# RMSNorm and SiLU on 64 tiles: float32 tiles on one SyncE queue, Square and Silu on ScalarE, rstd by a power on GpSimd

**Chip, cores, metric.** One core of one Trainium2 chip. The metric is the device time of one execution in microseconds; a kernel's figure is the median of its runs. Engines are named as the profile names them: ACT is ScalarE, DVE is VectorE, POOL is GpSimd, SP is SyncE.

## The reference

```python
# x: (8, 1024, 2048) float32, gamma: (2048,) float32, eps = 1e-5
rms = np.sqrt(np.mean(x ** 2, axis=-1, keepdims=True) + eps)
out = gamma * x / rms
return (out * (1 / (1 + np.exp(-out)))).astype(np.float32)
```

Both kernels cut the 8192 rows into 64 tiles of 128 rows (one per partition) by 2048, 1 MiB each in HBM.

## The kernel before

POOL issues every DMA, and the DMA casts between float32 in HBM and bf16 in SBUF (the page counts 512 KB for a load and 1024 KB for a store; HBM reads 68.16 MB and writes 67.11). DVE multiplies by gamma and sums squares, ACT takes the root, DVE the reciprocal, ACT the Silu. (In the cuts of code here `...` and left-out lines, such as the allocation of small tiles, stand in full in the kernel.)

```python
    pool = ctx.enter_context(tc.tile_pool(name="pool", bufs=8))
    ...
    for i in range(ntiles):
        xt = pool.tile([P, d], bf16)
        nc.gpsimd.dma_start(out=xt[:ts], in_=x2[s:e])          # casts
        xg = pool.tile([P, d], bf16)
        nc.vector.tensor_mul(out=xg[:ts], in0=xt[:ts], in1=g[:ts])
        nc.vector.tensor_tensor_reduce(...)                     # ss = sum of squares
        nc.scalar.activation(out=rms[:ts], in_=ss[:ts], func=Sqrt, ...)
        nc.vector.reciprocal(out=rstd[:ts], in_=rms[:ts])
        ot = pool.tile([P, d], bf16)
        nc.scalar.activation(out=ot[:ts], in_=xg[:ts], func=Silu, scale=rstd[:ts])
        nc.gpsimd.dma_start(out=o2[s:e], in_=ot[:ts])          # casts back
```

## Time and profile before

| | kernel before |
|---|---|
| time, median | 339.02 us (337.41 to 339.48, 4 runs) |
| span of the profile | 336.1 us |

The lines of the profile, and how I read them, are in the prediction. In short, the DMA bounds this kernel: the packets of its one queue fill 104% of sixteen engines' span, and no compute engine passes 66%.

### The profile page before, as it was taken

The page shows a single profiled execution, that of the slowest core. Times are in us where ns is not written, and L with a number is a line of the kernel's source. Part 1 is how long each engine was busy: PE and PEld are TensorE (multiplying, and loading weights), DVE is VectorE, ACT ScalarE, POOL GpSimd, SP SyncE. Part 2 cuts the span into 40 slices and gives each one's busy share as a digit, 9 for nine tenths or more (in the row PEclk, how much of TensorE's full clock was granted, in tenths as well). Part 3 has the DMA queues.
Part 4 walks back from the last instruction along what each step waited for, and adds up shares of the span by engine and source line. Part 5 has one row for each costly group of instructions (what it writes and reads, how often), then busy time and mean ns, then how long its engine had stood idle before and what let it go on. Part 6 is the DMA issues. An engine that isn't in the chain of part 4 may idle for free.

```text
span 336.1 us, 838 instructions
## 1 busy us (share of the span) xinstructions
DVE 221.2 (66%) x257; ACT 219.1 (65%) x188; POOL 69.0 (21%) x133
## 2 busy tenths in 40 slices
DVE  0999990407999914099999030899991308999900
ACT  1486977522869795238697761386978613869792
POOL 6012111050111110501111105011111050111110
DMA  7999999899999998999999989999999799999997
GB/s 140 212 214 254 335 398 363 332 312 208 214 288 327 402 365 321 324 214 214 291 316 414 366 325 310 214 212 319 307 424 367 286 297 214 213 311 309 420 429 273
DMA packets 18582, 101.24 MB, mean 301 GB/s; under 512 B 2064, under 2 KB 2064, under 8 KB 10384
## 3 DMA queue, kind: packets, MB, share of 16 engines
q0 software_dynamic: 18576, 101.20, 104.1%
q14 instruction: 6, 0.05, 0.0%
HBM read 68.16 MB, written 67.11 MB: 402 GB/s over the span
## 4 chain that ended last, share of the span: by engine, by line
issue 72%; POOL 14%; DMA 11%; POOLq 1%; PEldq 0%
DMA xt<-in_x_dram 11%; POOL out_dram L65 10%; POOL xt L42 4%; POOLq L65 0%; POOL g L34 0%; POOLq L96 0%; POOLq L42 0%; PEldq L96 0%
## 5 line engine op out<-in xcount | busy, mean ns | idle before, releaser
L48 DVE CUSTOM_DVE_ANT_0 xt<-xt 128x2048 bf16<-128x2048 bf16 x64 | 144.8, 2280 | 0.3
L45 DVE TENSOR_TENSOR xg<-xt,g 128x2048 bf16<-128x2048 bf16 x64 | 76.6, 1217 | 95.7 <-DMA xt<-in_x_dram 95.7
L62 ACT ACTIVATE ot<-xg,rstd 128x2048 bf16<-128x2048 bf16 x64 | 124.4, 1993 | 5.8 <-DVE rstd L59 5.5
L55 ACT ACTIVATE rms<-ss,eps_t 128x1 f32<-128x1 f32 x64 | 17.8, 292 | 101.8 <-DVE ss L48 63.7
L65 POOL DMA_DIRECT2D out_dram<-ot x64 | 34.2, 534 | 221.4 <-ACT ot L62 221.4
L42 POOL DMA_DIRECT2D xt<-in_x_dram x64 | 34.1, 554 | 38.8 <-DVE ss L48 22.8
L55 ACT ACT_TABLE_LOAD x30 | 38.5, 1283 | 2.1 <-DVE ss L48 1.0
L62 ACT ACT_TABLE_LOAD x30 | 38.5, 1283 | 0.5
L59 DVE RECIPROCAL rstd<-rms 128x1 f32<-128x1 f32 x64 | 8.6, 153 | 8.4 <-ACT rms L55 8.4
L48 DVE DVE_READ_ACCUMULATOR2_ANT ss<- 128x1 f32 x64 | 5.2, 81 | 0.0
L34 POOL DMA_DIRECT2D g<-in_gamma_dram x1 | 0.7, 667 | 0.8 <-PEq L96 0.8
L36 DVE MEMSET eps_t<- 128x1 f32 x1 | 0.1, 59 | 0.8 <-PEq L82 0.8
L82 POOL MEMSET const-float32-0.0<- 128x1 f32 x1 | 0.1, 99 | 0.2 <-issue 0.2
L82 POOL MEMSET const-bfloat16-1.0<- 128x1 bf16 x1 | 0.1, 102 | 0.0
L82 POOL MEMSET const-float32-1.0<- 128x1 f32 x1 | 0.1, 99 | 0.0
L82 POOL MEMSET const-uint8-127<- 128x1 uint8 x1 | 0.1, 99 | 0.0
## 6 DMA issues: line engine op xcount, KB each, us to landing
out_dram<-ot POOLq DMA_DIRECT2D x64, 1024.0 KB, 11.5
xt<-in_x_dram POOLq DMA_DIRECT2D x64, 512.0 KB, 15.5
g<-in_gamma_dram POOLq DMA_DIRECT2D x1, 512.0 KB, 4.7
```

The costliest lines, as they stand in the source:

```text
L34: nc.gpsimd.dma_start(out=g, in_=gbc)
L36: nc.vector.memset(eps_t, float(eps))
L42: nc.gpsimd.dma_start(out=xt[:ts], in_=x2[s:e])
L45: nc.vector.tensor_mul(out=xg[:ts], in0=xt[:ts], in1=g[:ts])
L48: nc.vector.tensor_tensor_reduce(out=xt[:ts], in0=xt[:ts], in1=xt[:ts], scale=1.0, scalar=0.0, op0=mybir.AluOpType.mult, op1=mybir.AluOpTy ...
L55: nc.scalar.activation(out=rms[:ts], in_=ss[:ts], func=mybir.ActivationFunctionType.Sqrt, scale=1.0 / d, bias=eps_t[:ts])
L59: nc.vector.reciprocal(out=rstd[:ts], in_=rms[:ts])
L62: nc.scalar.activation(out=ot[:ts], in_=xg[:ts], func=mybir.ActivationFunctionType.Silu, scale=rstd[:ts])
L65: nc.gpsimd.dma_start(out=o2[s:e], in_=ot[:ts])
L82: nc = _bacc.Bacc("TRN2", target_bir_lowering=False, num_devices=1)
```

## The change

The intent: keep the DMA engines full from end to end. Tiles stay float32, no DMA casts, and SyncE issues them all; 23 buffers are worked on in place; 16 loads run ahead; Square with a running sum replaces DVE's sum; the root becomes a power of -0.5 on POOL, so ACT loads no Sqrt table between two Silus (the kernel before has 60 table loads of 1.283 us, the changed one two). The text keeps Square two tiles ahead of Silu.

```diff
-        nc.gpsimd.dma_start(out=xt[:ts], in_=x2[s:e])
...
+    BUFS, LEAD = 23, 16
+    def load(i):
+        xt = pool.tile([P, d], f32, name="xt")
+        nc.sync.dma_start(out=xt, in_=x2[i * P:(i + 1) * P])
+        xts[i] = xt
...
+    nc.gpsimd.partition_broadcast(g, grow)        # gamma: one row, then all partitions
...
+    def stats(i):
+        nc.scalar.activation(out=sq, in_=xts[i], func=ACT.Square, accum_out=ss)
+        nc.gpsimd.tensor_scalar(out=var, in0=ss, scalar1=1.0 / d, scalar2=float(eps),
+                                op0=ALU.mult, op1=ALU.add)
+        nc.gpsimd.tensor_tensor(out=rstd, in0=var, in1=half, op=ALU.pow)
+    def scale(i):
+        nc.vector.scalar_tensor_tensor(out=xts[i], in0=xts[i], scalar=rstds.pop(i), in1=g,
+                                       op0=ALU.mult, op1=ALU.mult)
+    def finish(i):
+        nc.scalar.activation(out=xt, in_=xt, func=ACT.Silu)
+        nc.sync.dma_start(out=o2[i * P:(i + 1) * P], in_=xt)
+        if i + LEAD < ntiles:
+            load(i + LEAD)
+    for i in range(ntiles + 2):
+        if i < ntiles:
+            stats(i)
+        if 0 <= i - 1 < ntiles:
+            scale(i - 1)
+        if i >= 2:
+            finish(i - 2)
```

More of the change, by code (lines that the diff above doesn't have):

```diff
@@ L7 @@
 from concourse._compat import with_exitstack
+ACT = mybir.ActivationFunctionType
+ALU = mybir.AluOpType
 @with_exitstack
@@ L25 @@
     n, d = x2.shape
-    ntiles = (n + P - 1) // P
+    ntiles = n // P
+    BUFS, LEAD = 23, 16
     singles = ctx.enter_context(tc.tile_pool(name="singles", bufs=1))
-    pool = ctx.enter_context(tc.tile_pool(name="pool", bufs=8))
+    pool = ctx.enter_context(tc.tile_pool(name="pool", bufs=BUFS))
     small = ctx.enter_context(tc.tile_pool(name="small", bufs=8))
-    g = singles.tile([P, d], bf16)
-    gbc = bass.AP(tensor=gamma.tensor, offset=gamma.offset, ap=[[0, P], gamma.ap[0]])
-    nc.gpsimd.dma_start(out=g, in_=gbc)
@@ L35 @@
-    eps_t = singles.tile([P, 1], f32)
-    nc.vector.memset(eps_t, float(eps))
-    for i in range(ntiles):
-        s, e = i * P, min((i + 1) * P, n)
-        ts = e - s
-        xt = pool.tile([P, d], bf16)
-        nc.gpsimd.dma_start(out=xt[:ts], in_=x2[s:e])
-        xg = pool.tile([P, d], bf16)
-        nc.vector.tensor_mul(out=xg[:ts], in0=xt[:ts], in1=g[:ts])
-        ss = small.tile([P, 1], f32)
-        nc.vector.tensor_tensor_reduce(
-            out=xt[:ts], in0=xt[:ts], in1=xt[:ts],
-            scale=1.0, scalar=0.0,
-            op0=mybir.AluOpType.mult, op1=mybir.AluOpType.add,
-            accum_out=ss[:ts],
-        )
-        rms = small.tile([P, 1], f32)
-        nc.scalar.activation(out=rms[:ts], in_=ss[:ts],
-                             func=mybir.ActivationFunctionType.Sqrt,
-                             scale=1.0 / d, bias=eps_t[:ts])
-        rstd = small.tile([P, 1], f32)
-        nc.vector.reciprocal(out=rstd[:ts], in_=rms[:ts])
-        ot = pool.tile([P, d], bf16)
-        nc.scalar.activation(out=ot[:ts], in_=xg[:ts],
-                             func=mybir.ActivationFunctionType.Silu,
-                             scale=rstd[:ts])
-        nc.gpsimd.dma_start(out=o2[s:e], in_=ot[:ts])
@@ new lines @@
+    xts = {}
+    def load(i):
+        xt = pool.tile([P, d], f32, name="xt")
+        nc.sync.dma_start(out=xt, in_=x2[i * P:(i + 1) * P])
+        xts[i] = xt
+    grow = singles.tile([1, d], f32)
+    nc.sync.dma_start(out=grow, in_=bass.AP(tensor=gamma.tensor, offset=gamma.offset, ap=[[d, 1], gamma.ap[0]]))
+    g = singles.tile([P, d], f32)
+    nc.gpsimd.partition_broadcast(g, grow)
+    half = singles.tile([P, 1], f32)
+    nc.gpsimd.memset(half, -0.5)
+    sq = singles.tile([P, d], bf16)
@@ new lines @@
+    for i in range(LEAD):
+        load(i)
+    rstds = {}
+    def stats(i):
+        ss = small.tile([P, 1], f32, name="ss")
+        nc.scalar.activation(out=sq, in_=xts[i], func=ACT.Square, accum_out=ss)
+        var = small.tile([P, 1], f32, name="var")
+        nc.gpsimd.tensor_scalar(out=var, in0=ss, scalar1=1.0 / d, scalar2=float(eps),
+                                op0=ALU.mult, op1=ALU.add)
+        rstd = small.tile([P, 1], f32, name="rstd")
+        nc.gpsimd.tensor_tensor(out=rstd, in0=var, in1=half, op=ALU.pow)
+        rstds[i] = rstd
@@ new lines, in scale @@
+    def scale(i):
+        nc.vector.scalar_tensor_tensor(out=xts[i], in0=xts[i], scalar=rstds.pop(i), in1=g,
+                                       op0=ALU.mult, op1=ALU.mult)
+    def finish(i):
+        xt = xts.pop(i)
+        nc.scalar.activation(out=xt, in_=xt, func=ACT.Silu)
[9 more added lines that the diff above has]
+            finish(i - 2)
```

## The prediction

The sum came to 2.4 + 313.6 + 2.4 + 1 = 319.4 us of span, and with 3.3 more to 322.7 of time. The 1 for ramp and small dips was an allowance of mine, not a measurement.

> **What bounds the kernel now.** I read the page first, for shares and bytes.
>
> ```profile
> span 336.1 us, 838 instructions
> ...
> DVE 221.2 (66%) x257; ACT 219.1 (65%) x188; POOL 69.0 (21%) x133
> ...
> q0 software_dynamic: 18576, 101.20, 104.1%
> ...
> HBM read 68.16 MB, written 67.11 MB: 402 GB/s over the span
> ```
>
> No compute engine passes 66%, but the packets of the one DMA queue fill 104% of sixteen engines' span (packets overlap a little, so "full" reads above 100%). The 101 MB counts a load at its bf16 size in SBUF; HBM sees float32 both ways, 135.3 MB. To see whether 402 GB/s is the most there is, I cut the span into stretches; the columns are the stretch, its length, busy time of DVE, ACT and POOL, a clock that plays no part here, DMA share, and GB/s.
>
> ```profile
> 0.00:2.40 2.40, 0.06 (x1) 1.28 (x1) 1.34 (x6) 1.00 0.00 0
> 12.00:24.00 12.00, 11.66 (x16) 9.79 (x9) 2.13 (x4) 1.00 1.06 213
> 64.00:66.00 2.00, 0.00 (x0) 1.99 (x2) 0.00 (x0) 1.00 0.79 295
> 66.00:68.00 2.00, 0.00 (x0) 2.00 (x2) 0.53 (x1) 1.00 0.24 94
> 316.00:328.00 12.00, 3.62 (x8) 10.77 (x9) 1.59 (x3) 1.00 1.12 428
> 332.00:334.00 2.00, 0.00 (x0) 0.00 (x0) 0.00 (x0) 1.00 0.82 307
> 334.00:336.00 2.00, 0.00 (x0) 0.00 (x0) 0.00 (x0) 1.00 0.00 0
> ```
>
> 12 to 24 us holds loads only: 213 GB/s at the bf16 side is 426 GB/s read from HBM. 316 to 328 us holds stores only: 428 GB/s. So the ceiling is about 428 GB/s on the float32 side in either direction, or 1,048,576 B / 428 GB/s = 2.45 us for a tile, either way. The bytes alone need 135.27 MB / 428 = 316.1 us of the 336.1. The other 20 us are a head of 2.4 us without DMA, a tail (the last packet ends near 333.7, so 2.4 us), and dips. The dip at 64 to 68 us comes four times, about every 67 us. With 1.08 as a full share it loses 2 x (1.08-0.79)/1.08 + 2 x (1.08-0.24)/1.08 = 2.1 us; the same sum over 132:136, 198:202 and 264:268 (shares 0.24 and 0.67; 0.61 and 0.49; 0.84 and 0.05) gives 2.3, 2.0 and 2.4, together 8.8 us. About 6 us are left for smaller dips beside them. Why the dips come, the chain of waits tells less well than the waits and the timeline of POOL, which issues every DMA:
>
> ```profile
> POOL out_dram L65 <- ACT ot L62: 221.4, 64, 10.6
> DVE xg L45 <- DMA xt<-in_x_dram: 95.7, 14, 14.0
> ```
>
> ```profile
> 55.44 0.53 POOL L65 DMA_DIRECT2D out_dram<-ot  x1 [1.36 <-ACT ot L62]
> 66.56 0.53 POOL L65 DMA_DIRECT2D out_dram<-ot  x1 [10.58 <-ACT ot L62]
> 68.45 0.53 POOL L65 DMA_DIRECT2D out_dram<-ot  x1 [1.36 <-ACT ot L62]
> 68.97 3.72 POOL L42 DMA_DIRECT2D xt<-in_x_dram  x7
> ```
>
> POOL stood 10.6 us at a store whose Silu was not done, with seven loads behind it in program order, and meanwhile the sixteen engines ran dry. The 221 us of POOL waiting mostly cost nothing; only these ends do.
>
> [...]here rows have 8 KiB, and no trace yet shows a SyncE stream. [...]1993 ns for 2048 elements with a pointer scale[...], and loads of 1283.[...]
>
> ```profile
> L48 DVE CUSTOM_DVE_ANT_0 xt<-xt 128x2048 bf16<-128x2048 bf16 x64 | 144.8, 2280 | 0.3
> L45 DVE TENSOR_TENSOR xg<-xt,g 128x2048 bf16<-128x2048 bf16 x64 | 76.6, 1217 | 95.7 <-DMA xt<-in_x_dram 95.7
> ...
> L62 ACT ACTIVATE ot<-xg,rstd 128x2048 bf16<-128x2048 bf16 x64 | 124.4, 1993 | 5.8 <-DVE rstd L59 5.5
> ...
> L62 ACT ACT_TABLE_LOAD x30 | 38.5, 1283 | 0.5
> ```
>
> **The change, part by part.** *Bytes.* HBM traffic stays: 64 tiles of 1 MiB in, 64 out, 134.2 MB. Only gamma's read shrinks, from 128 copies of the row (1 MiB, 2.45 us) to one of 8 KB. At 428 GB/s: 134.2 / 0.428 = 313.6 us. This term is the prediction; the rest decides whether it is reached.
>
> *Removed.* 60 table loads (77 us of ACT) less the two that stay in the compiled order, 64 Sqrt (17.8), 64 Reciprocal and the DVE square-sums. All of it lay beside the DMA and gains nothing by itself.
>
> *Added, off the path.* DVE gets one float32 multiply-by-two[...]: like L48, about 2.29 us x 64 = 147 us. ACT gets Square and Silu without pointers[...]. POOL gets two instructions on 128x1 per tile[...]. Per tile the DMA needs 4.90 us[...], DVE 2.29[...]: the DMA still bounds.
>
> *Moved.* SyncE issues 16 loads, then store i and load i+16 by turns. In the compiled order each DMA waits for the one eight issues before it, in both kernels, so at most eight are in flight: 8 x 2.45 = 19.6 us of work ahead of the engines. The wait for a free tile (load i+16 wants store i-7, fourteen issues back) is then always already met. What is left is the wait for Silu. A tile lands about twelve pairs, 59 us, before its store comes up, so the stall of POOL above has no counterpart, and the four dips and their small neighbours (about 15 us) go. That is the gain.
>
> *Start.* First load packet as before near 2.4 us; sixteen loads last until 2.4 + 16 x 2.45 = 41.6 us, by which store 0 must be issued.[...]
>
> *End.* The last load is followed by 16 stores, 39 us of queued work.[...]
>
> *Sum.* Head 2.4 + bytes 313.6 + tail 2.4 + ramp and small dips 1 = 319.4 us of span. The quoted time lies 339.43 - 336.15 = 3.3 us above the span, so 322.7; I say 322.
>
> **Rivals.** *The SyncE path is slower per byte.*[...] About one in ten. *ACT becomes the bound.*[...] Against it: the 1993 ns of the trace is already with a pointer. *POOL starts late or is slow per tile.* Each microsecond by which store 0 comes after 41.6 us is a microsecond of time[...]. Between Square i and Silu i ACT has four other passes, 8 us, to hide POOL and DVE; pow and the sum scaling would have to take over 5 us together[...] to be felt. *More than expected:* SyncE starts sooner than POOL and the stream never dips: span 317, time 320.
>
> **Range and chances.** [...]The upper end, 332, lets the rate fall to 416 or the start lose 9 us. The border of "faster" is 339.43 x 0.98 = 332.6, so it takes nearly the whole first rival, or one of the others, to miss it: faster 0.87, same 0.10, slower 0.03.
>
> **What would show it right or wrong.** Right: stretches of 60 us in the middle at 426 to 430 GB/s without a dip; SyncE waiting for earlier DMAs and hardly for Silu; ACT under 80% busy with two table loads; first store issued before 41 us. Wrong: a steady rate under 420 (first rival); SyncE waiting for Silu in the middle and ACT above 90% (second); a hole in the DMA row near 42 us with POOL busy before it (third).

## More of the kernel before

The program text is not the order in which an engine works. A scheduler at build time decides for each engine in which order its instructions stand, and the build can list it.

## The result, and the profile after

The changed kernel takes 412.7 us (412.53 to 412.92, 4 runs) against 339.02: 22% slower, ratio 1.2185 (95% interval 1.2154 to 1.2215). Ratios here are the mean time of one kernel's fast runs over that of the other's of the same rounds, so not quite the ratio of the quoted medians. The range of 316 to 332 was missed by 81 us.

The page of the changed kernel: first the span, then the engines, then GB/s in 40 slices of 10.3 us each, now with both directions counted in float32.

```profile
span 410.8 us, 895 instructions
...
DVE 150.4 (37%) x64; ACT 244.6 (60%) x194; POOL 60.1 (15%) x134
...
GB/s 308 419 424 422 416 426 427 425 428 426 427 428 427 428 426 428 427 428 428 428 427 428 365 303 298 300 312 281 295 179 165 112 194 102 204 102 166 140 136 171
```

For 22 slices the DMA runs at its ceiling, as predicted (427 GB/s from 88 to 224 us). Then the rate falls to about 300 and at last to about 150 GB/s. No engine is busy: ACT, the busiest, has 60%. Something waits. Stretches of the same kernel (columns as in the prediction) date it:

```profile
40.00:80.00 40.00, 26.16 (x12) 40.00 (x33) 8.26 (x22) 1.00 1.01 424
100.00:200.00 100.00, 33.12 (x15) 54.95 (x43) 10.33 (x28) 1.00 1.01 427
...
312.00:400.00 88.00, 28.23 (x12) 48.06 (x38) 8.85 (x24) 1.00 0.35 145
```

At 40 to 80 us ACT has no gap. At 100 to 200 it is 55% busy, and so it stays to the end. The DMA doesn't feel it for another 136 us, because it still has work in stock: the break is at 88 us, its bill comes from 224 us on. By 88 us eighteen Silus were done and only thirteen stores issued; by 224 us the stock is gone, with 38 of each. The timeline shows what changed. First a tile in the good stretch (start, length, engine, line, operation, and in brackets what the engine waited for before):

```profile
52.31 1.89 ACT L59 ACTIVATE sq<-xt 128x2048 bf16<-128x2048 f32 x1
...
54.20 1.89 ACT L73 ACTIVATE xt<-xt 128x2048 f32<-128x2048 f32 x1
...
55.23 2.35 DVE L68 SCALAR_TENSOR_TENSOR xt<-xt,rstd,g 128x2048 f32<-128x2048 f32 x1 [1.34 <-POOL rstd L64]
...
56.00 1.89 ACT L59 ACTIVATE sq<-xt 128x2048 bf16<-128x2048 f32 x1
```

Square, Silu, Square follow one another on ACT every 3.69 us a tile, and DVE's multiply runs beside them. Then a tile after the break:

```profile
206.40 1.89 ACT L59 ACTIVATE sq<-xt 128x2048 bf16<-128x2048 f32 x1
...
208.20 0.19 ACT L59 ACTIVATION_READ_ACCUMULATOR sq<-xt 128x1 f32 x1
208.47 0.19 POOL L61 TENSOR_SCALAR var<-ss 128x1 f32<-128x1 f32 x1 [6.31 <-ACT sq L59]
208.75 0.55 POOL L64 TENSOR_TENSOR rstd<-var,half 128x1 f32<-128x1 f32 x1
209.33 2.35 DVE L68 SCALAR_TENSOR_TENSOR xt<-xt,rstd,g 128x2048 f32<-128x2048 f32 x1 [4.78 <-POOL rstd L64]
211.72 1.91 ACT L73 ACTIVATE xt<-xt 128x2048 f32<-128x2048 f32 x1 [3.33 <-DVE xt L68]
213.53 1.89 ACT L59 ACTIVATE sq<-xt 128x2048 bf16<-128x2048 f32 x1
```

Now everything stands in a row: Square, the sum's readout, POOL twice, DVE's multiply, Silu, and only then the next Square. From start to start: 1.80 for Square to its readout, 0.27 to POOL, 0.28 to the power, 0.58 to the multiply, 2.39 to Silu, 1.81 to the next Square, together 7.13 us. The DMA needs 4.90 for the same tile. This also gives the two steps of the fall: a load and a store of 1 MiB every 7.13 us are 294 GB/s (290 measured from 240 to 304 us), and after the last load, issued at 292 us, a store alone is 147 (145 measured).

The list of ACT's instructions in the compiled program says why, and the trace has the same order. For the first tiles it reads Square i+2, Silu i, by turns. Then come Silu of tiles 16, 17 and 18 in a row, and from there Square 19, Silu 19, Square 20, Silu 20, to the end, with one exception at tiles 34 and 35. The text asked for two Squares ahead; the scheduler let that lead go and never took it back. ACT did not start Square 20 while Silu 19, ahead of it, waited for DVE: tile 20's load was issued at 49.22 us and no DMA of this run took over 20.4 us to land, so the tile lay ready from 70 us on at the latest; ACT stood idle for 3.33 us before Silu 19 and started Square 20 only behind it, at 96.27.

The waits agree (who waited for whom, us in total, times, longest; the last line is SyncE's own queue):

```profile
DVE xt L68 <- POOL rstd L64: 252.9, 62, 23.7
ACT xt L73 <- DVE xt L68: 154.0, 46, 9.2
ACT sq L59 <- DMA xt<-in_x_dram: 5.6, 4, 4.1
...
SPq L74 <- ACT xt L73: 203.4, 34, 6.7
```

Square hardly ever waits for a load (5.6 us in all): the data was there. Silu waits 154 us for DVE, 43 waits of 3.33 (one of 3.46) making up most of it, and SyncE stands 203 us at stores whose Silu isn't done, just what POOL did in the kernel before and for a new reason.

### The profile page after: what moved, and what is told of

It reads as the page before. It is cut to its first block, busy times and chain, and to the rows that moved or that the text cites. A ratio compares the mean times of both kernels' runs of the same rounds, so it can differ in the third digit from the quotient of the medians.

```text
span 410.8 us, 895 instructions
## 1 busy us (share of the span) xinstructions
DVE 150.4 (37%) x64; ACT 244.6 (60%) x194; POOL 60.1 (15%) x134
## 3 DMA queue, kind: packets, MB, share of 16 engines
HBM read 67.12 MB, written 67.11 MB: 327 GB/s over the span
## 4 chain that ended last, share of the span: by engine, by line
issue 76%; POOL 10%; DVE 1%; ACT 0%; POOLq 0%
POOL rstd L64 7%; POOL var L61 3%; DVE xt L68 1%; ACT xt L73 0%; POOLq L64 0%; POOLq L115 0%; ACT sq L59 0%
## 5 line engine op out<-in xcount | busy, mean ns | idle before, releaser
L68 DVE SCALAR_TENSOR_TENSOR xt<-xt,rstd,g 128x2048 f32<-128x2048 f32 x64 | 150.4, 2352 | 253.7 <-POOL rstd L64 252.9
L73 ACT ACTIVATE xt<-xt 128x2048 f32<-128x2048 f32 x64 | 121.7, 1905 | 155.1 <-DVE xt L68 154.0
L59 ACT ACTIVATE sq<-xt 128x2048 bf16<-128x2048 f32 x64 | 121.2, 1894 | 5.7 <-DMA xt<-in_x_dram 5.6
L61 POOL TENSOR_SCALAR var<-ss 128x1 f32<-128x1 f32 x64 | 20.4, 319 | 327.6 <-ACT sq L59 316.1
L64 POOL TENSOR_TENSOR rstd<-var,half 128x1 f32<-128x1 f32 x64 | 37.0, 579 | 5.4 <-POOL var L61 0.2
L59 ACT ACTIVATION_READ_ACCUMULATOR sq<-xt 128x1 f32 x64 | 11.9, 186 | 0.0
L47 POOL PARTITION_BROADCAST g<-grow x1 | 2.3, 2302 | 8.2 <-issue 8.2
## 6 DMA issues: line engine op xcount, KB each, us to landing
xt<-in_x_dram SPq DMA_DIRECT2D x64, 1024.0 KB, 19.6
```

What stands on the lines that cost most here:

```text
L47: nc.gpsimd.partition_broadcast(g, grow)
L59: nc.scalar.activation(out=sq, in_=xts[i], func=ACT.Square, accum_out=ss)
L61: nc.gpsimd.tensor_scalar(out=var, in0=ss, scalar1=1.0 / d, scalar2=float(eps), op0=ALU.mult, op1=ALU.add)
L64: nc.gpsimd.tensor_tensor(out=rstd, in0=var, in1=half, op=ALU.pow)
L68: nc.vector.scalar_tensor_tensor(out=xts[i], in0=xts[i], scalar=rstds.pop(i), in1=g, op0=ALU.mult, op1=ALU.mult)
L73: nc.scalar.activation(out=xt, in_=xt, func=ACT.Silu)
```

## The experiments

Theory A: the order on ACT lays the chain POOL, DVE bare in every tile from 19 on. Theory B: POOL and DVE hold each other up, or ACT is too slow for two passes. Theory C: loads queue behind waiting stores on the one SyncE queue, and more loads ahead or a second queue would be the cure. All kernels give the reference's result unless said otherwise. The kernel before took 338.81 us beside the first four (one chip) and 337.70 beside the last four (another).

| run | time, us | ratio to before | expected, us |
|---|---|---|---|
| e1_keep | 323.01 | 0.954 | 322 |
| e2_lead1 | 323.08 | 0.954 | 322 if hidden |
| e3_lead0 | 483.77 | 1.429 | 485 |
| e4_replay_pow | 446.10 | 1.316 | 439 |
| e5_dma_only | 321.93 | 0.953 | 321 |
| e6_before_pin | 326.04 | 0.965 | 324 |
| e7_keep_sqrt | 439.25 | 1.300 | 469 |
| e8_lead20 | 397.48 | 1.177 | 395 |

**e1_keep: pin the order of the text.** A pin is an edge at build time that keeps an instruction behind the one traced before it on its engine; ACT's order in this run's trace is that of the text. It adds no instruction (895 with it and without) and no wait that shows (e3_lead0, below).

```diff
-        nc.scalar.activation(out=sq, in_=xts[i], func=ACT.Square, accum_out=ss)
+        tc.keep_in_program_order(nc.scalar.activation(out=sq, in_=xts[i], func=ACT.Square, accum_out=ss))
...
-        nc.scalar.activation(out=xt, in_=xt, func=ACT.Silu)
+        tc.keep_in_program_order(nc.scalar.activation(out=xt, in_=xt, func=ACT.Silu))
```

> The changed kernel with one difference: ScalarE's passes are pinned to the order of the program text, Square i+2 ahead of Silu i for every tile. Theory A (the order that the build gave ScalarE after tile 18, Square i directly followed by Silu i, lays POOL's and DVE's work bare in every tile, 7.13 us instead of the DMA's 4.90): the time falls from 412.7 to 322 (318 to 327), DMA at 426 to 430 GB/s to the end. Theory B (POOL and DVE hold each other up[...], or ACT's two passes are too slow): the order alone helps little, over 370. Theory C (one in-order SyncE queue lets loads queue behind stores that wait): no help, over 390.

Measured: 323.01 us (322.85 to 323.45), faster than before by 4.6%. The same instructions in another order save 90 us. Its page, SyncE's waits, and a stretch of its timeline:

```profile
span 321.1 us, 895 instructions
...
DVE 150.4 (47%) x64; ACT 242.3 (75%) x194; POOL 54.8 (17%) x134
```

```profile
SPq L74 <- DMA out_dram<-xt: 118.3, 56, 2.6
...
SPq L74 <- ACT xt L73: 2.4, 4, 1.7
```

```profile
202.68 1.91 ACT L59 ACTIVATE sq<-xt 128x2048 bf16<-128x2048 f32 x1 [1.10 <-DMA xt<-in_x_dram]
...
204.58 1.89 ACT L73 ACTIVATE xt<-xt 128x2048 f32<-128x2048 f32 x1
```

Busy times are nearly as before the pin. Behind the first tile Silu no longer waits for DVE; a tile takes ACT 3.69 us up to about tile 35 and then, with Square waiting for its load, about 4.90, the DMA's period. SyncE waits for earlier DMAs (in the compiled order each waits for the one eight issues before it; in the changed kernel a load lands 19.6 us after its issue in the median, eight times 2.45), and only 2.4 us for Silu. Theory C falls here: the order of loads and stores on SyncE is the same in both traces, and one queue suffices. So does the strong form of theory B.

**e2_lead1 and e3_lead0: how much lead is needed.** The same pins, with Square one tile ahead of Silu, or not at all. The cut is e3_lead0; e2_lead1 has `ntiles + 1`, `scale(i)` and `finish(i - 1)`:

```diff
-    for i in range(ntiles + 2):
+    for i in range(ntiles + 0):
         if i < ntiles:
             stats(i)
-        if 0 <= i - 1 < ntiles:
-            scale(i - 1)
-        if i >= 2:
-            finish(i - 2)
+        scale(i)
+        finish(i)
```

> Pinned as in e1_keep, but only Square i+1 stands ahead of Silu i. Theory A: between the end of Square i and Silu i stand Silu i-1 and Square i+1, 3.8 us plus the readout, and the chain var, pow, multiply takes about 3.4 us with its hops (7.13 less two passes and a readout), so it is just hidden: ACT about 4 us per tile, DMA bounds, 322 (318 to 330). If POOL's first instruction is held up by DVE (1 to 2.5 us instead of 0.19, seen in the first 45 us of the changed kernel), it is not hidden: 5 to 6 us per tile, 330 to 400.

> The opposite: Square i, its chain and Silu i in a row for all 64 tiles, pinned. Theory A: all 64 tiles at 7.13 us: first Silu near 26, 63 x 7.13 = 449, last Silu, store and end 8, plus 2 between span and time: 485 (478 to 492). Theories B and C have no reason to go above 413.

Measured: 323.08 and 483.77 us. With no lead every tile takes 7.13 us, and 63 steps of 7.13 are the 449 us between the first Silu at 27.6 and the last at 476.8. A lead of one hides the chain as well as two. In e2_lead1 nothing holds POOL up either (its sum takes 0.19 us on the mean, 0.24 in e1_keep, 0.32 in the changed kernel), and the time is that of e1_keep, so POOL's hold-ups cost nothing that shows. The price of the missing lead is now known from three doses: none, 44 and 63 steps of 7.13 us from Silu to Silu give 323, 413 and 484 us. The pins themselves cost nothing here: the step is 7.13 us in e3_lead0 with them and in the changed kernel without.

**e4_replay_pow: make the chain longer on an idle engine.** ACT's order as the changed kernel had it, written out and pinned, and a power of 1.0 on POOL more:

```diff
+        nc.gpsimd.tensor_tensor(out=same, in0=var, in1=one, op=ALU.pow)   # one = 1.0
...
-        nc.gpsimd.tensor_tensor(out=rstd, in0=var, in1=half, op=ALU.pow)
+        nc.gpsimd.tensor_tensor(out=rstd, in0=same, in1=half, op=ALU.pow)
...
+    lead = [3] + [2] * 15 + [2, 1, 0] + [0] * 15 + [1] + [0] * 29
+    q = 0
+    for i in range(ntiles):
+        while q < min(ntiles, i + 1 + lead[i]):
+            stats(q)
+            scale(q)
+            q += 1
+        finish(i)
```

> ScalarE's order of the changed kernel exactly, written out and pinned, and one more power of 128x1 (to 1.0, result unchanged) on POOL between sum and rstd. Theory A: the 44 or 45 tiles with no lead each get longer by one such instruction, 0.55 to 0.58 us: 412.7 + 26 = 439 (434 to 443), though POOL is only 15% busy. Theory C: the DMA order is untouched, 413. Theory B: about 413 to 420, POOL's added work lies clear of DVE's.

Measured: 446.10 us, 33 more than the changed kernel. It was run at another time. Only theory A expected a rise of this kind; the size is 7 us over what I expected. The timeline of this kernel, from one Silu to the next:

```profile
201.41 1.91 ACT L77 ACTIVATE xt<-xt 128x2048 f32<-128x2048 f32 x1 [3.95 <-DVE xt L72]
...
206.20 0.55 POOL L68 TENSOR_TENSOR rstd<-same,half 128x1 f32<-128x1 f32 x1
...
209.17 1.91 ACT L77 ACTIVATE xt<-xt 128x2048 f32<-128x2048 f32 x1 [3.95 <-DVE xt L72]
```

The period is 7.76 us, 0.63 above 7.13, since the added power costs 0.55 and the hop to the next instruction 0.08. From Silu of tile 18 to that of tile 63 pass 344.9 us instead of 316.9, so 28.0 of the 33. The rest is in the start: the first Silu comes 2.0 us later and the first eighteen steps take 3.5 more. No run has the written-out order without the added power. POOL, busy 15% of the time in the changed kernel, sets the end: what counts is that its instruction lies in a bare chain.

**e5_dma_only: the floor.** No arithmetic on tiles, so a wrong result; every store waits only for its own load.

> The changed kernel without any arithmetic on the tiles (wrong result on purpose): SyncE loads and stores in the same order, each store waiting only for its own load. Theory A says that e1_keep already stands on the DMA's floor: 134.2 MB / 428 GB/s = 313.6, a head of 2.2 and an end of 2.6 as in e1_keep, 319 of span, 321 of time (319 to 323.5), so that compute costs e1_keep under 3 us. If compute still costs e1_keep something in its middle, this one is under 317.

Measured: 321.93 us. e1_keep, on another chip, is 1.1 us above a kernel that computes nothing on its tiles; by their ratios to the kernel before beside each, 0.954 and 0.953, the two can't be told apart. At most about a microsecond is left in its compute, with the DMAs in this order.

**e6_before_pin: the order of the DMAs, with four more buffers, in the kernel before.**

```diff
-    pool = ctx.enter_context(tc.tile_pool(name="pool", bufs=8))
+    pool = ctx.enter_context(tc.tile_pool(name="pool", bufs=12))
...
+    def load(i):
+        xt = pool.tile([P, d], bf16, name="xt")
+        tc.keep_in_program_order(nc.gpsimd.dma_start(out=xt, in_=x2[i * P:(i + 1) * P]))
...
+    for i in range(LEAD):           # LEAD = 11
+        load(i)
...
-        nc.gpsimd.dma_start(out=xt[:ts], in_=x2[s:e])
...
-        nc.gpsimd.dma_start(out=o2[s:e], in_=ot[:ts])
+        tc.keep_in_program_order(nc.gpsimd.dma_start(out=o2[s:e], in_=ot[:ts]))
+        if i + LEAD < ntiles:
+            load(i + LEAD)
```

> The kernel before with one idea of the change alone, the order of the DMAs: POOL's queue is pinned to eleven loads and then store i and load i+11 by turns, pools of 12 buffers instead of 8; bf16 tiles, cast in the DMA, table loads and DVE work stay. If what e1_keep gains over the kernel before comes from the order of the DMAs (the four stalls of POOL), this one gains nearly the same: 316.1 for the bytes, 2.4 + 2.4 for the ends, 1, and 2 between span and time: 324 (321 to 329). If it comes from float32 tiles on SyncE, this one stays at 335 to 340.

Measured: 326.04 us, ratio 0.965. Against its own rounds it gains 11.7 us; e1_keep gains 15.8 against its rounds. POOL's waits for Silu at its stores, 221.4 us with a longest of 10.6 in the kernel before, are down to 20.7 and 4.1. So three quarters of what the change was after is to be had in the kernel before, with bf16 tiles, the cast and the table loads all kept, by the order of the DMAs and four more buffers. (The two came together in this run; which of them does more is open.) Of the other 4 us, gamma's 1 MiB would be 2.45 by my estimate, from 428 GB/s: its row is no longer read 128 times, and HBM reads 67.12 MB in the changed kernel for 68.16 in the kernel before.

**e7_keep_sqrt: was the power on POOL needed?** e1_keep with Sqrt on ACT and reciprocal on DVE in place of POOL's two instructions.

> e1_keep with rstd as in the kernel before: Sqrt on ScalarE and reciprocal on DVE instead of the two POOL instructions. The order pinned for Square and Silu makes two table loads per tile: 1.89 + 1.89 + 0.19 + 0.29 + 2 x 1.28 = 6.83 us of ScalarE per tile, above the DMA's 4.90: 26 + 64 x 6.83 + 6 = 469 (455 to 485). If that holds, the power on POOL is what lets Square live on ScalarE; if the time is near 323, it made no difference.

Measured: 439.25 us. The answer is yes for this order: ACT is 97% busy, and its row shows what fills it.

```profile
DVE 160.9 (37%) x129; ACT 422.7 (97%) x381; POOL 2.6 (1%) x6
...
200.90 1.28 ACT L63 ACT_TABLE_LOAD   x1
202.19 0.30 ACT L63 ACTIVATE rms<-ss,eps_t 128x1 f32<-128x1 f32 x1
202.51 1.28 ACT L74 ACT_TABLE_LOAD   x1
203.80 1.91 ACT L74 ACTIVATE xt<-xt 128x2048 f32<-128x2048 f32 x1
```

A tile takes 6.73 us of ACT, close to the 6.83 expected. I was off by 30 us. Twenty of them are in the start: I took the 26 us of the first Silu over from the changed kernel, but here ACT works from 6.1 us on nearly without a gap, since its root doesn't wait for POOL. Twelve are in ACT's passes, which take 425 us (6.1 to 431.3) and not 64 x 6.83 = 437; the 1.8 us between span and time, not counted, go the other way. An order that takes the roots of several tiles between two table loads, as the kernel before does with its 60 loads for 64 tiles, was not run with Square on ACT, so it isn't shown that the root must leave ACT.

**e8_lead20: more loads ahead, nothing pinned.**

```diff
-    BUFS, LEAD = 23, 16
+    BUFS, LEAD = 23, 20
```

> The changed kernel with 20 loads ahead instead of 16, nothing pinned. In its compiled order Square runs ahead of Silu for the first 23 tiles instead of 18, and then Square i and Silu i alternate again. Theory A: five tiles fewer at 7.13 instead of 3.69 us: 412.7 - 17 = 395 (388 to 403). If the cure were more loads ahead (Theory C), it should come near 323.

Measured: 397.48 us. The break moves back from tile 19 to tile 24, five tiles for four more loads, and it stays. A build without a run shows the same: with 8 loads ahead the lead is gone from about tile 9 on. The scheduler holds the lead while prefetched tiles last. That it then expects the loads to land later than they do, and so prefers a Silu that is ready, is what I think; it is not shown.

## Why the prediction was wrong, point by point

- *What bounds the kernel before, and the DMA's ceiling of 428 GB/s:* right. The first rival, a slower SyncE path, fell: the changed kernel ran at 427 from 100 to 200 us.
- *Bytes, head and tail, 319.4 us of span and 322.7 of time:* right for what it described. The kernel described, with the order of the text, is e1_keep, with 321.1 and 323.0. That the time fits to 0.3 us is luck: the span was 1.7 us too low, and the 3.3 us from span to time, a median against the span of one execution, are 1.8 in e1_keep.
- *Work per tile:* ACT 3.82 us busy (244.6 / 64), with 1.89 for Square, 1.90 for Silu and 0.19 for the readout (Silu with a pointer, on bf16 tiles, took 1.99 in the kernel before); DVE 2.35 for 2.29; POOL 0.19 and 0.55 where nothing held it up. All lie below the DMA's 4.90.
- *Start:* the first load was issued at 1.1 us, where POOL issued its first at 1.9 in the kernel before. POOL waited 8.2 and 11.2 us before and behind its broadcast of 2.3 us (see the last section), its statistics began at 22.5 us, and store 0 was issued at 28.0, 13.6 us before the 41.6 of the prediction. There is no hole in the DMA at 42: 414 GB/s from 40 to 48 us.
- *"Between Square i and Silu i ACT has four other passes, 8 us, to hide POOL and DVE":* **this step failed.** It holds for the first tiles only. From tile 19 on, tiles 34 and 35 apart, there is no pass between them, and 3.33 us of waiting are added to the 3.8 of ACT's work: 7.13 per tile. I had the compiled order, took the number of table loads and SyncE's waits from it, and read ACT's pattern off its first rows and the text.
- *"A tile lands about twelve pairs, 59 us, before its store comes up, so the stall of POOL above has no counterpart":* it fell with that step. The tile had landed, but its Silu came late: SyncE stood 203 us. (The store that a load's buffer needs is fifteen issues back, not fourteen; nothing hangs on it.)
- *The rivals:* "ACT becomes the bound" had the right place, the wrong cause. I asked only how long ACT's work is; with 3.82 us per tile it lies below the DMA's 4.90, and yet its period was 7.13, 3.33 of it waiting for DVE. My test for this rival, ACT above 90% busy, would have cleared it. What theory B names shows as a few long sums on POOL (0.7 to 2.4 us for 0.19, last section); they cost nothing that shows, as e2_lead1, where the sum takes 0.19 on the mean, and e1_keep, 0.24, are 0.07 us apart.

## What to carry to other kernels

On ACT here the position of an instruction in the list became time: 7.13 us a tile with no lead, 3.69 with a lead of two until the DMA's 4.90 set the pace. Where two passes of one engine on one tile have other engines' work between them, count how many passes on other tiles stand between them, in the compiled list, from the first row to the last, and not in the program text. A share of busy time did not rule ACT out as the limit (it was 60%); compare an engine's period per tile with the bound's (7.13 against 4.90). Where a schedule must hold, pin it, and run the same kernel without arithmetic to know when to stop.

## What else the traces show of POOL, ACT and the DMA

POOL in the changed kernel and then in e7_keep_sqrt (start, length, instruction, and what POOL waited for):

```profile
9.00 2.30 POOL L47 PARTITION_BROADCAST g<-grow  x1 [8.18 <-issue]
22.52 0.45 POOL L61 TENSOR_SCALAR var<-ss 128x1 f32<-128x1 f32 x2 [11.22 <-issue]
...
24.27 1.82 POOL L61 TENSOR_SCALAR var<-ss 128x1 f32<-128x1 f32 x1
```

```profile
2.35 2.29 POOL L47 PARTITION_BROADCAST g<-grow  x1 [1.54 <-DMA grow<-in_gamma_dram]
```

- In the changed kernel POOL stood 8.2 us before the broadcast and 11.2 us after it, when its sums and powers followed. Its queue has a MODIFY_POOL_CONFIG near the start of each wait, at 1.0 and at 11.2 us. Where the broadcast was POOL's last work, that first wait is missing: in e7_keep_sqrt it started at 2.35 us, as soon as gamma had landed, after a wait of 1.5, and in e5_dma_only it lies between 2.2 and 8 us. Why the first wait goes is open.
- Small instructions on POOL: 0.19 us for multiply and add on 128x1, 0.55 for a power (medians of e1_keep).
- The third sum above took 1.82 us instead of 0.19 and ended at 26.09, as DVE's multiply (23.69 to 26.04) did. In the changed kernel five sums up to 40 us and one at 200 us took 0.7 to 2.4 us; in the bare chain after the break they take 0.19. That DVE's multiply holds the sum up is how I read these times; no run tests it alone.
- In e7_keep_sqrt a table load takes 1.28 us and the next instruction starts 1.29 us after the load does (200.90 and 202.19), so a switch costs 1.29 us there.
- Loads and stores mixed, issued by SyncE in rows of 8 KiB, ran at 426 (e5_dma_only, 8 to 310 us) to 428 GB/s (e1_keep, 240 to 310 us).
